# Grouped-query attention on one core: casts of two heads at a time, placed in gaps of GpSimd's plan

## The chip, the core and the metric

The kernel runs on one core of a Trainium2 chip. Its time is the device time in microseconds, here the median of three runs. A core has five engines with queues of their own: TensorE (PE in the profile, its weight loads PEld), VectorE (DVE), ScalarE (ACT), GpSimd (POOL) and SyncE (SP), which here only issues transfers. Each engine runs its own instructions in order; semaphores order them among each other.

## The reference

Batch 8, 8 heads of q, 2 key groups (k and v), 1024 rows, head size 64, all float32. Four heads of q share a group:

```python
scores = scale * np.matmul(q_group, k_group.transpose(0, 1, 3, 2))
scores_max = np.max(scores, axis=-1, keepdims=True)
attn = np.exp(scores - scores_max)
attn = attn / (np.sum(attn, axis=-1, keepdims=True) + 1e-08)
output[:, q_start:q_end, :, :] = np.matmul(attn, v_group)
```

## The kernel before

There are 64 jobs, j = 0 to 63: one head of q of one batch each. A job has eight pairs of score matmuls (L853), each of which fills a slot of 128 x 1024 float32 in PSUM; there are three slots. The exponential of a slot is made by one of two engines. ScalarE does it in one activation (L863, "act"). VectorE does it in steps: a linear pass out of PSUM into 16-bit integers whose bits are a rough exponential (L874, "dpass"), then, over a chain of two such slots (2048 columns), the mantissa bits (L881, "zh"), the exponent bits (L888, "two") and a product that corrects the mantissa (L897, "mul"). The exponent part `et` and the corrected part `zt` then both enter the second matmul with v (L915, "pv"). In the last TAIL heads a fourth step (L902, "add") adds the two on VectorE, so that TensorE needs one matmul per tile there and not two. Each group of seven pieces of the result is divided by its sums on VectorE (reciprocal L980, multiplication L989) and stored by SyncE (L993).

How many of a head's eight slots VectorE takes at most is its quota (L150): `FIRST[j]` for the first heads, then `MXD` and one more where `j % MORE == MORE // 2`.

The order of all of this is written out before the kernel is built. `Plan` plays the engines against each other with fixed costs (the `M_` constants in nanoseconds: `M_ACT` is one activation) and, where TensorE has a choice, plays each alternative `HORIZON` nanoseconds ahead and takes the one with the least idle time of ScalarE and VectorE. The events of the plan, sorted by planned time, become the instructions of each engine in that order.

GpSimd takes a part of the product step off VectorE. `Plan.gpsimd` (L208) does this only beside VectorE's pass out of PSUM (and the normalisation that may follow it): it opens a window of that length, first lets in a placement of v (`gplace`, L654) if one is due, then as many columns of a waiting product as fit (`gmul`, L827), at most `GWINS` parts per chain, for chains of heads 2 to 58. The rest of the columns stays with VectorE (L897). Each part waits for the VectorE instruction issued just before the window, so that it doesn't start sooner (L830). The plan itself counts no cast.

The matmuls need q and k transposed and in bfloat16. For this GpSimd issues transfers that cast one head of q (`cast_q`, L621) or one key group (`cast_k`, L634) from float32 in HBM to a bfloat16 tensor `qd` or `kd` in HBM, 128 KB each; SyncE then issues a transposing transfer of it into SBUF (`turn_q`, `turn_k`), 11 us and 12.5 us ahead of the first use by the plan. A cast is due 18 us (q) or 19 us (k) ahead (L762, L769). Once GpSimd's parts have begun, a due cast goes into the list `casts`. It leaves it right after a part if the next part with a later planned time starts over 2300 ns after this one's planned time, or, when it is 3000 ns overdue, at whatever event comes next. In both cases it waits for the score matmul that was last put in order (L809). The lines that decide this:

```python
    begun = [e[0] for e in ev if e[1] in ("gmul", "gplace")]
...
        if casts and casts[0][0] < when - 3000:
            cast(*casts.pop(0)[1:])
...
            later = [t for t in begun if t > when]
            if casts and (not later or later[0] > when + 2300):
                cast(*casts.pop(0)[1:])
```

Of the kernel before, what the change touches and what calls it, by code (L numbers as in the profile page):

```python
# [23 lines left out]
M_SWITCH = 99  # L24
M_MM = 30.3
M_PVTAIL = 180
M_ACT = 923
M_ATAIL = 107
M_FIX = 66
M_DTAIL = 80  # L30
# [6 lines left out]
M_GLEAD = 160  # L37
M_GFIX = 120
M_GCOL = 2.09
# [2 lines left out]
M_NORM = 531  # L42
M_HOLD = 2500
M_SPARE = 500

M_GAP = 90
M_RUNWAY = 1800
# [1 line left out]
M_WAIT = 250  # L49
M_TOL = 300  # L50

HORIZON = 8000
W_A = 1.0
W_D = .28
W_P = 0
# [1 line left out]
INF = float("inf")  # L57
# [1 line left out]
NPIECE = 8  # L59
GRAIN = 3  # L60
MXD = 2
MORE = 5
TAIL = 3
CHN = 2
LONG = 6
FIRST = (2, 1, 1)
GWINS = 2
GFROM = 2
GTO = 5
# [64 lines left out]
class Plan:  # L134
# [5 lines left out]
    def __init__(self, nj, npt, nct, nyt):  # L140
# [8 lines left out]
        self.qready = [M_START] + [M_START + M_Q1 + M_QSTEP * j for j in range(nj - 1)]  # L149
        self.quota = [FIRST[j] if j < len(FIRST) else MXD + (j % MORE == MORE // 2) for j in range(nj)]  # L150
        s = State()
# [42 lines left out]
    def act(self, s):  # L194
# [5 lines left out]
        else:  # L200
            _, sl, j, c = s.aq.pop(0)
            s.note(t, "act", sl, j, c)
            s.idleA += t - s.endA
            s.tA = s.endA = t + M_ACT
            s.slot[sl] = s.tA + M_ATAIL + M_SEE
# [33 lines left out]
    def dve(self, s):  # L239
# [13 lines left out]
        elif s.dq and s.dq[0][0] <= t and not (norm and t - s.norms[0][0] > M_HOLD):  # L253
            _, sl, j, c = s.dq.pop(0)
            n = len(STEPS) if j >= nj - TAIL else 3
            if s.open and s.open.nsteps != n:
# [23 lines left out]
        else:  # L280
# [5 lines left out]
            for ch in s.chains:  # L286
# [3 lines left out]
                if ch.at == 2 and ch.nsteps == 3 and ch.cols and ch.wins < GWINS:  # L290
                    if GFROM <= ch.pairs[0][0] < nj - GTO:
                        if s.dq and s.dq[0][0] < t + M_SPARE:
                            continue
# [47 lines left out]
    def choices(self, s):  # L341
# [10 lines left out]
        free = [x for x in (0, 1, 2) if s.slot[x] <= t]  # L352
        runway = s.tA - t + M_ACT * len(s.aq)
        slack = runway - cold * M_PAIR - M_PTAIL - (M_SWITCH if s.mode != "s" else 0)
# [70 lines left out]
    def pe(self, s, kind):  # L425
        t, nj = s.tP, self.nj
        if kind in "AD":
# [12 lines left out]
            else:  # L440
                s.dcount[j] += 1
                if j == 0:
                    s.twice.append(c)
                if j < nj - TAIL:
                    s.mms[j] += 1
# [78 lines left out]
    def run(self, s):  # L524
        while not s.end:
# [3 lines left out]
            kind, others = self.choices(s)  # L529
            if others and HORIZON:  # L530
                best = self.cost(s.copy(), kind, t + HORIZON)
                for x in others:
                    c = self.cost(s.copy(), x, t + HORIZON)
                    if c < best - 1:
# [8 lines left out]
def kernel(  # L543
# [7 lines left out]
    nc = tc.nc  # L551
    FP32 = mybir.dt.float32
    BF16 = mybir.dt.bfloat16
# [5 lines left out]
    B, H, S, D = q.shape  # L559
    G = k.shape[1]  # L560
# [3 lines left out]
    HS = S // 2  # L564
    NJ = B * H
# [12 lines left out]
    dram = ctx.enter_context(tc.tile_pool(name="dram", bufs=1, space=bass.MemoryType.DRAM))  # L578
# [39 lines left out]
        nc.vector.memset(t[:, :, :, D : D + 1], 1.0)  # L618
    kt, qt, qd, kd, vs = {}, {}, {}, {}, {}

    def cast_q(j):  # L621
        b, h = divmod(j, H)
        t = dram.tile([HS, 2 * D], BF16, name=f"qd{j}")
        qd[j] = t
        if j == NJ - 1:
            return nc.gpsimd.dma_start(
                out=t.rearrange("(c p) d -> p c d", p=128), in_=rows(q[b, h], True)
            )
        return nc.gpsimd.dma_start(  # L629
            out=t.rearrange("(a x) d -> a (x d)", x=4),  # L630
            in_=q[b, h].rearrange("(a x) d -> a (x d)", x=8),
        )

    def cast_k(b, g):  # L634
        t = dram.tile([HS, 2 * D], BF16, name=f"kd{b}_{g}")
        kd[(b, g)] = t
        return nc.gpsimd.dma_start(  # L637
            out=t.rearrange("(a x) d -> a (x d)", x=4),
            in_=k[b, g].rearrange("(a x) d -> a (x d)", x=8),
        )  # L640

    def rows(x, fours=False):
        how = "(p c two) d -> p c (two d)" if fours else "(c p two) d -> p c (two d)"
        return x.rearrange(how, p=128, two=2)
# [49 lines left out]
    load(nc.sync, "k", 1, NH)  # L696
    load_v(0, 0)
    cast_q(1)
    make_identity(nc, ident)
    cast_q(2)  # L700

    new_bank(0)
# [37 lines left out]
    for c in range(NH):  # L740
        for half in range(2):
            lo = half * D
# [4 lines left out]
    h = HS // 2  # L747
# [7 lines left out]
    ev = list(plan.ev)  # L755
    n = len(ev)
    for j in range(NJ):
        b, h = divmod(j, H)
        at = need[j]
        g = h // HPG  # L760
        if h % HPG == 0 and j:
            ev.append((at - 19000, "ck", None, (b, g), None))  # L762
            ev.append((at - 12500, "tk", None, (b, g), None))
            ev.append((at - 4000, "cp", None, (b, g), None))
            ev.append((places[j // HPG] - 8000, "lv", None, (b, g), None))
        if j == 0:
            ev.append((M_START + 100, "pl", None, (b, g), None))
        if j > 2:
            ev.append((at - 18000, "cq", None, j, None))  # L769
        if j > 1:  # L770
            ev.append((at - 11000, "tq", None, j, None))
    for x in [e for e in plan.ev if e[1] == "norm"]:
        lo, hi = x[2]
# [9 lines left out]
    now = None  # L783
# [3 lines left out]
    def flat(t):  # L787
        return t.bitcast(BF16).rearrange("p i a b -> p (i a b)")

    def terms(j, par, only=range(NC)):  # L790

        for ci in only:
            c = ci if par == 0 else (ci + NH) % NC
            if (j, c) in where:
                ch, i = where[(j, c)]
                if j < NJ - TAIL:
                    yield ci, et[ch].bitcast(BF16)[:, i, par, :]
# [1 line left out]
            elif (j, c) in pt:  # L799
                yield ci, pt[(j, c)][:, par, :]  # L800

    begun = [e[0] for e in ev if e[1] in ("gmul", "gplace")]
    casts = []
    vec, gps = None, None

    def cast(kind, j):
        ins = cast_k(*j) if kind == "ck" else cast_q(j)
        if now:
            tc.add_manual_dep(ins.ins, now.ins.name, Sync, reason="loads in time, not sooner")  # L809

    for when, kind, x, j, c, *cols in ev:
        if casts and casts[0][0] < when - 3000:
            cast(*casts.pop(0)[1:])
        if kind in ("ck", "cq"):

            if gps is None:
                cast(kind, j)
            else:
                casts.append((when, kind, j))
        elif kind in ("gmul", "gplace"):  # L820
# [3 lines left out]
            else:  # L824
                lo, w = c
                z = flat(zt[j])[:, lo : lo + w]
                gps = nc.gpsimd.tensor_tensor(  # L827
                    out=z, in0=flat(yt[j])[:, lo : lo + w], in1=z, op=ALU.mult
                )
            tc.add_manual_dep(gps.ins, vec.ins.name, Sync, reason="VectorE needs the port before")  # L830

            later = [t for t in begun if t > when]
            if casts and (not later or later[0] > when + 2300):
                cast(*casts.pop(0)[1:])
        elif kind == "tk":
            turn_k(*j)
        elif kind == "cp":
# [7 lines left out]
        elif kind == "score":  # L845
            b, h = divmod(j, H)
            t = kt[(b, h // HPG)]
            where_s[(j, c)] = new_slot(x)

            for half in range(2):  # L850
                lo = half * D
                ci = (c + NH * half) % NC
                now = nc.tensor.matmul(  # L853
                    sps[x][:, half, :],
                    lhsT=t[lo : lo + D, c // NH, ci % NH * 128 : (ci % NH + 1) * 128],
                    rhs=qt[j][lo : lo + D, 0, :],
                    start=True,
                    stop=True,
                )
# [9 lines left out]
        elif kind == "dpass":  # L869
            ch, i = j  # L870
            where[c] = j
            if i == 0:
                yt[ch] = yp.tile([128, CHN, 2, HS], U16, name="yt")
            vec = nc.vector.tensor_scalar(  # L874
                out=yt[ch][:, i, :, :], in0=where_s[c],
                scalar1=EXP_A, scalar2=EXP_B, op0=ALU.mult, op1=ALU.add,
            )
        elif kind == "zh":
# [3 lines left out]
                out=zt[j][:, 0:c], in0=yt[j][:, 0:c], scalar1=0x7F, scalar2=0x3F00,  # L882
                op0=ALU.bitwise_and, op1=ALU.bitwise_or,
            )
        elif kind == "two":
# [3 lines left out]
                out=et[j][:, 0:c], in0=yt[j][:, 0:c], scalar1=0x7F80, scalar2=None,  # L889
# [5 lines left out]
        elif kind == "mul":  # L895
            z = flat(zt[j])[:, 0 : cols[0]]
            vec = nc.vector.tensor_tensor(  # L897
                out=z, in0=flat(yt[j])[:, 0 : cols[0]], in1=z, op=ALU.mult
            )
        elif kind == "add":  # L900
            z = zt[j].bitcast(BF16)[:, 0:c]
            vec = nc.vector.tensor_tensor(  # L902
                out=z, in0=et[j].bitcast(BF16)[:, 0:c], in1=z, op=ALU.add
            )
        elif kind == "pv":
            job, piece = divmod(x, NPIECE)
            b, h = divmod(job, H)
            qs, par = divmod(piece, 2)
            lo = (x - plan.groups[plan.group_of[x]][0]) * (D + 1)
# [14 lines left out]
        elif kind == "pvf":  # L924
# [4 lines left out]
            for i in range(NPIECE):  # L929
# [3 lines left out]
                lo = i % 4 * (D + 1)  # L933
# [9 lines left out]
        elif kind == "pvl":  # L943
            b, h = divmod(NJ - 1, H)
# [3 lines left out]
            for i in range(NPIECE):  # L948
# [4 lines left out]
                lo = i % 4 * (D + 1)  # L953
# [9 lines left out]
        elif kind in ("rec", "norm"):  # L963
            lo, hi = x
            n = hi - lo
# [24 lines left out]
        elif kind == "store":  # L990
            b, h = divmod(j, H)
            r = place_of(j * NPIECE)
            ins = nc.sync.dma_start(  # L993
                out=rows(out[b, h], j in (0, NJ - 1)),
                in_=ost[:, r : r + NPIECE, :].rearrange("p (s two) d -> p s (two d)", two=2),
# [32 lines left out]
```

## Time and profile before

| | |
|---|---|
| median of three runs | 362.16 us (362.12 to 362.54) |
| the profiled execution | 361.83 us, of which the span is 360.1 us |
| exponentials on ScalarE (L863) | 374, 346.7 us busy |
| passes on VectorE (L874) | 138, 167.3 us busy |
| products on GpSimd (L827) | 91, 101.8 us busy |
| casts of q (L626, L629) and of k (L637) | 63 and 15 |
| issue to landing of a cast | q 3.5 us, k 3.4 us (medians) |

The span runs from the first to the last instruction of the core; the time of a run is a little longer. Busy time counts an engine's instructions without double counting where one begins before the last has ended; the mean of one instruction therefore can be longer than the distance from one start to the next. Of VectorE that distance is the better price: its instructions overlap by about 0.08 us.

### The profile page before, as it was taken

Reading aid. Unit: us, or ns where it says so; the run is one execution under the profiler, and the core shown is the slowest. Engines: PE = TensorE matmul, PEld = TensorE weight load, DVE = VectorE, ACT = ScalarE, POOL = GpSimd, SP = SyncE. Lnnn points to the kernel's source line nnn. Section 1 sums busy time; section 2 is a strip of 40 time slices with the busy share of each in tenths; the row PEclk is TensorE's granted clock in tenths of the full one; section 3 lists DMA queues with packets and bytes.
Section 4 is the critical chain, followed back from the end, with each engine's and each line's share of the span. In section 5 each row is a group of like instructions: output and inputs, shape, how many; then the busy total and the mean of one; then the engine's idle time right before and its main releaser. Section 6 shows DMA issues by size and latency. Waiting matters only on the chain.

```text
span 360.1 us, 14126 instructions
## 1 busy us (share of the span) xinstructions
PE 349.0 (97%) x6214; PEld 222.7 (62%) x6214; DVE 350.8 (97%) x511; ACT 349.3 (97%) x378; POOL 156.0 (43%) x191
## 2 busy tenths in 40 slices
PE   8889999999999999999999999999999999999995
PEld 3456666666666666666666666666665666566664
DVE  4999999999999999999999999999999999999995
ACT  5999999999999999999999999999999999999993
POOL 4124452452544365562466554664545344342000
PEclk9999999999999999999999999999999999999999
DMA  8847595674747868487676866657487755854123
GB/s 191 131 84 125 105 191 122 105 135 103 164 102 130 167 99 161 97 136 165 114 120 119 165 133 111 148 111 144 94 120 144 180 98 88 158 120 76 46 60 120
DMA packets 89406, 44.83 MB, mean 125 GB/s; under 512 B 46000, under 2 KB 87600, under 8 KB 88112
## 3 DMA queue, kind: packets, MB, share of 16 engines
q1 hardware_dynamic: 86208, 33.44, 40.8%
q0 software_dynamic: 2992, 10.23, 21.7%
q8 instruction: 48, 0.79, 0.9%
q10 hardware_dynamic: 144, 0.26, 0.2%
q14 instruction: 14, 0.11, 0.1%
HBM read 25.17 MB, written 27.00 MB: 145 GB/s over the span
## 4 chain that ended last, share of the span: by engine, by line
DVE 65%; PE 30%; issue 4%; DVEq 0%
DVE yt L874 32%; PE ops L915 15%; PE sp L853 13%; DVE zt L897 11%; DVE et L888 7%; DVE ost L989 7%; DVE zt L881 6%; DVE rec L980 2%; PE ops L708 1%; DVE zt L902 1%; PE sp L955 1%; PE sp L731 0%; PE ops L743 0%; PE ops L731 0%; DVE warm L616 0%
## 5 line engine op out<-in xcount | busy, mean ns | idle before, releaser
L863 ACT ACTIVATE pt<-sp 128x1024 bf16<-128x1024 f32 x374 | 346.7, 1034 | 1.8 <-PE sp L853 1.1
L853 PE MATMUL sp<-qt,kt 64*128 64x512 bf16 x1024 | 175.0, 384 | 5.0 <-DVE yt L874 2.9
L915 PE MATMUL ops<-va,pt 128*128 128x65 bf16 x2896 | 177.3, 194 | 0.0
L874 DVE TENSOR_SCALAR yt<-sp 128x1024 uint16<-128x1024 f32 x138 | 167.3, 1212 | 0.8 <-PE sp L853 0.8
L915 PEld LDWEIGHTS <-pt 128*128 128x128 bf16 x2896 | 128.4, 97 | 37.8 <-issue 37.8
L827 POOL TENSOR_TENSOR zt<-yt,zt 128x416 bf16<-128x416 bf16 (+3 forms) x91 | 101.8, 1118 | 101.8 <-DVE zt L881 47.5
L915 PE MATMUL ops<-va,zt 128*128 128x65 bf16 x1072 | 126.4, 194 | 0.2 <-DVE zt L897 0.2
L915 PE MATMUL ops<-va,et 128*128 128x65 bf16 x1032 | 119.1, 194 | 0.0
L915 PEld LDWEIGHTS <-et 128*128 128x128 bf16 x1032 | 81.1, 98 | 20.3 <-issue 20.3
L915 PEld LDWEIGHTS <-zt 128*128 128x128 bf16 x1072 | 85.3, 97 | 13.5 <-issue 13.2
L853 PEld LDWEIGHTS <-kt 64*128 64x128 bf16 x1024 | 47.8, 93 | 54.6 <-issue 33.6
L897 DVE TENSOR_TENSOR zt<-yt,zt 128x960 bf16<-128x960 bf16 (+6 forms) x70 | 62.0, 887 | 0.0
L629 POOL DMA_DIRECT2D qd<-in_q_dram x62 | 36.6, 591 | 32.4 <-PE sp L853 27.5
L881 DVE TENSOR_SCALAR zt<-yt 128x2048 uint16<-128x2048 uint16 x70 | 46.7, 670 | 0.3
L888 DVE TENSOR_SCALAR et<-yt 128x2048 uint16<-128x2048 uint16 x70 | 46.4, 664 | 0.0
L989 DVE TENSOR_TENSOR ost<-ops,rec 128x448 f32<-128x448 f32 (+2 forms) x73 | 44.3, 607 | 0.2
L654 POOL CAST va<-vs 128x512 bf16<-128x512 f32 x16 | 9.8, 611 | 21.8 <-DVE ost L989 6.8
L637 POOL DMA_DIRECT2D kd<-in_k_dram x15 | 9.2, 612 | 14.5 <-PE sp L853 14.5
L980 DVE RECIPROCAL rec<-ops 128x7 f32<-128x7 f32 (+2 forms) x73 | 14.1, 193 | 0.0
L708 PE MATMUL ops<-warm 128*128 128x128 bf16 (+1 forms) x30 | 5.2, 311 | 1.7 <-DVE warm L616 1.2
L708 PEld LDWEIGHTS <-warm 128*128 128x128 bf16 x30 | 2.4, 111 | 5.1 <-issue 4.0
L902 DVE TENSOR_TENSOR zt<-et,zt 128x2048 bf16<-128x2048 bf16 (+1 forms) x4 | 4.3, 1072 | 0.0
(37 smaller groups left out, 24.7 us busy)
## 6 DMA issues: line engine op xcount, KB each, us to landing
out_dram<-ost SPq DMA_DIRECT2D x64, 256.0 KB, 2.9
qd<-in_q_dram POOLq DMA_DIRECT2D x63, 128.0 KB, 3.5
vs<-in_v_dram SPq DMA_DIRECT2D x16, 256.0 KB, 4.4
kd<-in_k_dram POOLq DMA_DIRECT2D x15, 128.0 KB, 3.4
kt<-kt SPq DMA_DIRECT2D x30, 64.0 KB, 3.5
qt<-qd SPq DMA_TRANSPOSE x63, 3.7
q<-in_q_dram ACTq DMA_DIRECT2D x1, 256.0 KB, 2.9
kt<-kd SPq DMA_TRANSPOSE x15, 4.3
```

Source lines behind the costliest of these rows:

```text
L629: return nc.gpsimd.dma_start(out=t.rearrange("(a x) d -> a (x d)", x=4), in_=q[b, h].rearrange("(a x) d -> a (x d)", x=8),)
L708: nc.tensor.matmul(ops[bank][:, lo : lo + cols], lhsT=warm[:, 0:128], rhs=warm[:, 0:cols], start=not beside, stop=True, skip_group_check=b ...
L827: gps = nc.gpsimd.tensor_tensor(out=z, in0=flat(yt[j])[:, lo : lo + w], in1=z, op=ALU.mult)
L853: now = nc.tensor.matmul(sps[x][:, half, :], lhsT=t[lo : lo + D, c // NH, ci % NH * 128 : (ci % NH + 1) * 128], rhs=qt[j][lo : lo + D, 0, ...
L863: exps.append(nc.scalar.activation(out=p, in_=where_s[(j, c)], func=AF.Exp, scale=scale))
L874: vec = nc.vector.tensor_scalar(out=yt[ch][:, i, :, :], in0=where_s[c], scalar1=EXP_A, scalar2=EXP_B, op0=ALU.mult, op1=ALU.add,)
L881: vec = nc.vector.tensor_scalar(out=zt[j][:, 0:c], in0=yt[j][:, 0:c], scalar1=0x7F, scalar2=0x3F00, op0=ALU.bitwise_and, op1=ALU.bitwise_or,)
L888: vec = ins = nc.vector.tensor_scalar(out=et[j][:, 0:c], in0=yt[j][:, 0:c], scalar1=0x7F80, scalar2=None, op0=ALU.bitwise_and,)
L897: vec = nc.vector.tensor_tensor(out=z, in0=flat(yt[j])[:, 0 : cols[0]], in1=z, op=ALU.mult)
L915: nc.tensor.matmul(ops[plan.group_of[x] % 2][:, lo : lo + D + 1], lhsT=p[:, qs * 128 : (qs + 1) * 128], rhs=va[(b * G + h // HPG) % NVA][: ...
L980: vec = nc.vector.reciprocal(out=to, in_=sums)
L989: vec = nc.vector.tensor_tensor(out=to, in0=o, in1=by, op=ALU.mult)
```

## The change

A cast takes two heads of q in one transfer: heads 1, 2 and 63 stay alone, and every odd j from 3 to 61 brings head j+1 with it. The two key groups of a batch come in one transfer too, apart from the first batch's. The transfer keeps 128 rows on each side, each twice as long; the two heads are slices of one tensor in HBM, and the transposes are unchanged.

Casts leave the list by another rule. After each part of GpSimd, the planned time at which GpSimd is free is worked out from that part's cost. While the planned start of the next part, whatever its time, is later than that by more than `M_ISSUE` (650 ns), a cast is issued there, without waiting for a score, and 650 ns are added. A cast that is more than 5000 ns overdue goes out at the next event, with the wait, as before.

The plan's constants change too, so the whole order is another one: `M_ACT`, `HORIZON`, the quotas (`MORE`, `FIRST`) and `TAIL`.

```diff
-M_ACT = 923
+M_ACT = 917
+M_ISSUE = 650
-HORIZON = 8000
+HORIZON = 5500
-MORE = 5
-TAIL = 3
+MORE = 6
+TAIL = 4
-FIRST = (2, 1, 1)
+FIRST = (2, 1)
...
+    def cast(src, t):
+        return nc.gpsimd.dma_start(
+            out=t.rearrange("(a x) d -> a (x d)", a=128),
+            in_=src.rearrange("(a x) d -> a (x d)", a=128),
+        )
+
     def cast_q(j):
         b, h = divmod(j, H)
-        t = dram.tile([HS, 2 * D], BF16, name=f"qd{j}")
-        qd[j] = t
         if j == NJ - 1:
+            t = qd[j] = dram.tile([HS, 2 * D], BF16, name=f"qd{j}")
             return nc.gpsimd.dma_start(
                 out=t.rearrange("(c p) d -> p c d", p=128), in_=rows(q[b, h], True)
             )
-        return nc.gpsimd.dma_start(
-            out=t.rearrange("(a x) d -> a (x d)", x=4),
-            in_=q[b, h].rearrange("(a x) d -> a (x d)", x=8),
-        )
+        n = 2 if j > 2 else 1
+        t = dram.tile([n * HS, 2 * D], BF16, name=f"qd{j}")
+        for i in range(n):
+            qd[j + i] = t[i * HS : (i + 1) * HS, :]
+        return cast(q.rearrange("b h s d -> (b h s) d")[j * S : (j + n) * S, :], t)
 
     def cast_k(b, g):
-        t = dram.tile([HS, 2 * D], BF16, name=f"kd{b}_{g}")
-        kd[(b, g)] = t
-        return nc.gpsimd.dma_start(
-            out=t.rearrange("(a x) d -> a (x d)", x=4),
-            in_=k[b, g].rearrange("(a x) d -> a (x d)", x=8),
-        )
+        n = G - g
+        t = dram.tile([n * HS, 2 * D], BF16, name=f"kd{b}_{g}")
+        for i in range(n):
+            kd[(b, g + i)] = t[i * HS : (i + 1) * HS, :]
+        lo = (b * G + g) * S
+        return cast(k.rearrange("b g s d -> (b g s) d")[lo : lo + n * S, :], t)
...
-            ev.append((at - 19000, "ck", None, (b, g), None))
+            if g == 0 or b == 0:
+                ev.append((at - 19000, "ck", None, (b, g), None))
...
-        if j > 2:
+        if j > 2 and (j % 2 or j == NJ - 1):
             ev.append((at - 18000, "cq", None, j, None))
...
-    begun = [e[0] for e in ev if e[1] in ("gmul", "gplace")]
+    begun = [e for e in ev if e[1] in ("gmul", "gplace")]
+    starts = [e[0] + M_GLEAD for e in begun] + [INF]
+    nth, free = 0, 0
...
-    def cast(kind, j):
+    def begin(kind, j, gate):
         ins = cast_k(*j) if kind == "ck" else cast_q(j)
-        if now:
+        if now and gate:
             tc.add_manual_dep(ins.ins, now.ins.name, Sync, reason="loads in time, not sooner")
...
-        if casts and casts[0][0] < when - 3000:
-            cast(*casts.pop(0)[1:])
+        if casts and casts[0][0] < when - 5000:
+            begin(*casts.pop(0)[1:], True)
...
-            later = [t for t in begun if t > when]
-            if casts and (not later or later[0] > when + 2300):
-                cast(*casts.pop(0)[1:])
+            took = 614 if kind == "gplace" else M_GFIX + M_GCOL * c[1]
+            free = max(free, when + M_GLEAD) + took
+            nth += 1
+            while casts and starts[nth] > free + M_ISSUE:
+                begin(*casts.pop(0)[1:], False)
+                free += M_ISSUE
```

More of the change, by code (lines that the diff above doesn't have):

```diff
@@ L800, in terms @@
                 yield ci, pt[(j, c)][:, par, :]
-    begun = [e[0] for e in ev if e[1] in ("gmul", "gplace")]
+    begun = [e for e in ev if e[1] in ("gmul", "gplace")]
+    starts = [e[0] + M_GLEAD for e in begun] + [INF]
+    nth, free = 0, 0
     casts = []
     vec, gps = None, None
-    def cast(kind, j):
+    def begin(kind, j, gate):
         ins = cast_k(*j) if kind == "ck" else cast_q(j)
-        if now:
+        if now and gate:
             tc.add_manual_dep(ins.ins, now.ins.name, Sync, reason="loads in time, not sooner")
     for when, kind, x, j, c, *cols in ev:
-        if casts and casts[0][0] < when - 3000:
-            cast(*casts.pop(0)[1:])
+        if casts and casts[0][0] < when - 5000:
+            begin(*casts.pop(0)[1:], True)
         if kind in ("ck", "cq"):
             if gps is None:
-                cast(kind, j)
+                begin(kind, j, True)
             else:
```

## The prediction

> **What bounds the kernel now.** I read the page's busy shares first. Three engines stand at 97% of the span, so the shares alone can't say which one sets the end:
>
> ```profile
> PE 349.0 (97%) x6214; PEld 222.7 (62%) x6214; DVE 350.8 (97%) x511; ACT 349.3 (97%) x378; POOL 156.0 (43%) x191
> ```
>
> Next the table of waits, for VectorE (DVE) and then ScalarE (ACT). Columns: who <- for whom, us in total, times, longest.
>
> ```profile
> DVE q L719 <- DMA q<-in_q_dram: 2.4, 1, 2.4
> ...
> DVE yt L874 <- PE sp L853: 0.8, 2, 0.5
> DVE rec L980 <- PE sp L955: 0.6, 1, 0.6
> ```
>
> ```profile
> ACT pt L863 <- PE sp L853: 1.1, 3, 0.6
> ```
>
> VectorE's waits all lie in the first 9 us, except the 0.6 us ahead of the last reciprocal. By the timeline it has no other gap of over 50 ns from 8.5 to 355.1 us. ScalarE's row of the page has 374 exponentials, 346.7 us busy, 0.927 us each. By their starts, nine in ten follow the last one after 0.90 to 0.93 us, 0.918 in the mean of these, so 374 x (0.927 - 0.918) = 3.4 us, plus its own 1.1 us of waits, is time in which ScalarE stood late, about 4.5 us. TensorE has slack that the busy share hides: by the starts of L853, some pairs of score matmuls come 0.39 us and more apart where an unhindered pair takes 0.22. So the end is set by the sum of VectorE's work; ScalarE could follow some 4.5 us sooner before it became the bound.
>
> Then VectorE's instructions by shape, to see whether its work runs at its own price. The product (L897) has these rows:
>
> ```profile
> L897 DVE TENSOR_TENSOR zt<-yt,zt 128x960 bf16<-128x960 bf16 x21 | 13.9, 661 | 0.0
> ...
> L897 DVE TENSOR_TENSOR zt<-yt,zt 128x1216 bf16<-128x1216 bf16 x9 | 6.9, 769 | 0.0
> ...
> L897 DVE TENSOR_TENSOR zt<-yt,zt 128x1248 bf16<-128x1248 bf16 x5 | 5.2, 1039 | 0.0
> ```
>
> 1248 columns cost 1039 ns where 1216 cost 769. That is no price of the shape: three of the five were held up. The timelines of GpSimd (POOL) and VectorE show by what. At 318 us:
>
> ```profile
> 317.55 0.61 POOL L654 CAST va<-vs 128x512 bf16<-128x512 f32 x1 [0.75 <-DVE et L888]
> 318.10 0.55 POOL L629 DMA_DIRECT2D qd<-in_q_dram  x1
> 318.67 0.92 POOL L827 TENSOR_TENSOR zt<-yt,zt 128x384 bf16<-128x384 bf16 x1
> ```
>
> ```profile
> 317.41 1.21 DVE L874 TENSOR_SCALAR yt<-sp 128x1024 uint16<-128x1024 f32 x1
> 318.54 0.61 DVE L989 TENSOR_TENSOR ost<-ops,rec 128x448 f32<-128x448 f32 x1
> 319.07 1.20 DVE L897 TENSOR_TENSOR zt<-yt,zt 128x1248 bf16<-128x1248 bf16 x1
> 320.19 1.21 DVE L874 TENSOR_SCALAR yt<-sp 128x1024 uint16<-128x1024 f32 x1
> ```
>
> The plan gave GpSimd one window (the PSUM pass L874 and the normalisation L989) for a placement of v and a product part. The cast of q was issued between the two, so the part ran from 318.67 to 319.59, past the window's end at 319.07, and VectorE's product took 1.12 us to the next start in place of 0.72.
>
> **What the Trainium skill says.** SBUF - State Buffer, "SBUF: two separate sides": VectorE and GpSimd share a pair of SBUF ports; an instruction of VectorE with two SBUF inputs or in a two-port mode, and one of GpSimd, exclude each other for the whole instruction. The trace agrees: L897 loses about 0.4 us beside a late part, L874 (PSUM input) keeps its 1.13 us beside 60 parts. DMA: Bandwidth & Descriptors, "SWDGE vs HWDGE vs iDMA": a cast in flight must be issued by GpSimd, which writes its descriptors into SBUF and is locked out in the same way. The trace agrees: casts take 486 ns alone and up to 900 ns beside VectorE's two-port work, while no instruction of VectorE is longer beside a cast alone. The same page, "Anatomy of one DMA": about 2.0 us plus bytes over 436 GB/s; doubling a cast from 128 to 256 KB written adds 0.3 us by that, to the 3.5 us to landing that the page shows.
>
> **Part by part.**
>
> *Collisions removed.* I went through all starts of L897, L881 and L888 and compared each with its shape's usual distance to the next start. Eight are late, each beside a product part that had been pushed back by a cast: L897 at 79.77 (+0.42), 257.50 (+0.22), 262.35 (+0.40), 271.22 (+0.42), 295.49 (+0.41) and 319.07 (+0.41), and L881 at 112.53 (+0.10) and 292.51 (+0.11). Sum 2.49 us. Of the 78 casts 18 are followed at once by a product; 8 of those cost something. The old rule leaves out a part with the same planned time (t > when), which is how a cast came between placement and product, and lets a late cast in anywhere, behind a TensorE score. The new one takes the next part by its index and asks for 650 ns of free plan. Between the 107 parts of GpSimd, 101 of 106 gaps are over 650 ns, the median 2.0 us, so few casts should grow 5 us old and fall back on the gated path. I take all eight as gone: -2.49 us, on VectorE, hence on the path.
>
> *Fewer casts.* q: heads 1, 2, 63 alone and 30 pairs, 33 for 63; k: 8 for 15. So 37 fewer of about 0.57 us, 21 us of GpSimd, which is 43% busy: worth nothing by itself. The price of a double cast isn't in the trace. It keeps 128 rows on each side, twice as long: at least 0.49 to 0.55 us as now, at most 1.1 if time goes with bytes. The cast of head 63 (L626), with more and shorter rows, took 0.81. I take 0.55; at 1.1 it would outrun 650 ns, and 30 of the 106 gaps lie between 0.65 and 1.1 us.
>
> *Waits and queues.* The casts lose their wait for a score (27.5 + 14.5 us for q and k), behind which only GpSimd's next parts queue. SyncE's transposes (63 + 15, unchanged) wait for casts 58.6 us now, and stores queue behind them; the only cost of this to TensorE is 0.4 us. A cast planned 18 us ahead and at most 5 late lands some 8 us before need. Nothing.
>
> *Split of heads.* Quotas for VectorE before: 2+1+1, then 2 each and 3 where j mod 5 is 2 (12 heads): 138. After: 2+1, then 2 each and 3 where j mod 6 is 3 (11 heads): 138. So 374 exponentials and 138 passes stay.
>
> *TAIL 4.* Heads 60 to 63 take the fourth step: 2+2+2+3 = 9 pairs in place of 7, one more addition (L902) of 2048 columns, +1.13 us from start to next start; TensorE drops 16 matmuls at 30 ns, 0.5 us. VectorE's one late gap (0.6 us) might absorb half. Between +0.5 and +1.13; I take +1.13.
>
> *New plan.* M_ACT 917 is nearer the 0.918 us seen than 923. The number of columns that GpSimd takes follows from the plan and can't be read from the trace: now 91 parts, 58 x 416 + 26 x 672 + 5 x 384 + 2 x 704 = 44,928 columns. One column is worth (1133 - 565) / (2048 - 960) = 0.52 ns of VectorE. The chains that may be shared (heads 2 to 58) have 124 pairs under both quotas. I take no change; +-5 parts of 494 columns is +-1.3 us.
>
> Sum: -2.49 + 1.13 = -1.4 us. Against the profiled execution's own 361.83 us (span 360.1 and 1.7 around it) that is 360.4; that execution is 0.33 us below the median of 362.16, so the forecast is 360.7 us. The 0.2% that can be told from no change is 0.7 us.
>
> **Rivals.** *More than that* (12%): ScalarE's late 4.5 us allow it, if the new plan also hands over some 5 parts more: 360.7 - 1.3 = 359.4. *It cancels* (17%): double casts cost near 1.1 us and outrun tight gaps, or late ones still fall into windows; four new collisions of 0.41 eat 1.4 us: 362.2. For it: 30 tight gaps, and casts stretch to 0.9 us beside VectorE even now. Against: there are half as many casts, each takes the first gap that is wide enough, and its overrun is only the part above 650 ns. *Slower* (26%): a shorter look-ahead (HORIZON 5500) and other quotas give an order with fewer shared windows in heads 2 to 58. From 5 to 6 lost parts (1.4 / 0.257) it is no gain, from 9 slower than the bound; a loss of 12 gives 360.7 + 12 x 494 x 0.52 ns = 363.8. For it: only 91 of at most 124 parts are used, so the number is loose, and the plan counts no cast, so nothing balances it against them; against: passes, pairs and window lengths are the same.
>
> **How the numbers follow.** Forecast 45% (360.0 to 361.4), more 12%, cancels 17%, slower 26%. Faster 0.57 is forecast and more together; same 0.17; slower 0.26. The range reaches from 358.8, at 7 to 8 parts gained, to 363.8, where 12 are lost.
>
> **What would show it.** Right: no L897 or L881 beside a late L827; about 41 casts, each behind a part and 0.5 to 0.6 us long; the row of L902 at four of 2048 columns; no new wait of VectorE. Wrong: L629 near 1 us with products at once behind; the columns of L827 well under 44,928; gaps of VectorE before L874; SyncE's late transposes stopping scores.

## The result and the profile after

The changed kernel takes 358.81 us (median of 4 runs, 357.89 to 359.50) against 362.14 us. The ratio is 0.9907, 95% interval 0.9882 to 0.9932: 3.3 us faster, where 1.4 were forecast. The profiled execution took 358.87 us, its span is 357.0. The page's first part after the change:

```profile
PE 345.1 (97%) x6196; PEld 221.2 (62%) x6196; DVE 347.9 (97%) x512; ACT 347.3 (97%) x378; POOL 149.8 (42%) x161
```

VectorE has one instruction more and 2.9 us less busy time. Its waits (who <- for whom, us, times, longest) are as few as before:

```profile
DVE q L724 <- DMA q<-in_q_dram: 2.9, 1, 2.9
DVE yt L885 <- PE sp L864: 1.0, 2, 0.5
DVE warm L617 <- PEq L1023: 0.9, 1, 0.9
DVE rec L991 <- PE sp L966: 0.3, 1, 0.3
```

So the time came out of VectorE's own work. (The second row's two waits are 0.5 us each, at 8.1 and 10.6 us; the later one is new.) The groups by shape (busy us, mean ns | idle before) show which:

```profile
L835 POOL TENSOR_TENSOR zt<-yt,zt 128x416 bf16<-128x416 bf16 x56 | 54.6, 974 | 56.3 <-DVE et L899 21.6 <-DVE zt L892 16.2 <-PE sp L864 5.4
L835 POOL TENSOR_TENSOR zt<-yt,zt 128x672 bf16<-128x672 bf16 x35 | 50.9, 1455 | 47.8 <-DVE et L899 30.5 <-DVE zt L892 9.0 <-DVE zt L908 4.3
...
L908 DVE TENSOR_TENSOR zt<-yt,zt 128x960 bf16<-128x960 bf16 x30 | 18.9, 630 | 0.0
...
L913 DVE TENSOR_TENSOR zt<-et,zt 128x2048 bf16<-128x2048 bf16 x4 | 4.8, 1202 | 0.0
L835 POOL TENSOR_TENSOR zt<-yt,zt 128x704 bf16<-128x704 bf16 x3 | 4.6, 1517 | 7.2 <-DVE rec L991 6.6 <-DVE et L899 0.6
L835 POOL TENSOR_TENSOR zt<-yt,zt 128x384 bf16<-128x384 bf16 x4 | 3.6, 909 | 0.0
L908 DVE TENSOR_TENSOR zt<-yt,zt 128x1248 bf16<-128x1248 bf16 x3 | 2.3, 780 | 0.0
```

GpSimd's parts are now 98, and more of them are wide: 56 x 416 + 35 x 672 + 3 x 704 + 4 x 384 = 50,464 columns, 5,536 more than the 44,928 before. Before, the first two of these rows were:

```profile
L827 POOL TENSOR_TENSOR zt<-yt,zt 128x416 bf16<-128x416 bf16 x58 | 56.4, 972 | 61.4 <-DVE et L888 24.3 <-DVE zt L881 23.5 <-DVE ost L989 6.7
L827 POOL TENSOR_TENSOR zt<-yt,zt 128x672 bf16<-128x672 bf16 x26 | 37.8, 1453 | 37.6 <-DVE zt L881 22.6 <-DVE et L888 13.6 <-DVE zt L897 1.4
```

At 0.52 ns a column the difference is 2.9 us less for VectorE. The held-up products are gone too: 1248 columns take 780 ns where their mean was 1039, 960 take 630 where it was 661. The fourth addition of 2048 columns (L913) is there, at 1.13 us from start to start.

But three other VectorE instructions are held up now, by 1.07 us in all. At 250 us, GpSimd and then VectorE in the timeline:

```profile
250.60 0.61 POOL L659 CAST va<-vs 128x512 bf16<-128x512 f32 x1 [3.56 <-DMA vs<-in_v_dram]
```

```profile
250.71 1.04 DVE L892 TENSOR_SCALAR zt<-yt 128x2048 uint16<-128x2048 uint16 x1
251.68 1.21 DVE L885 TENSOR_SCALAR yt<-sp 128x1024 uint16<-128x1024 f32 x1
```

A placement of v began outside its window, as soon as its load had landed, and the mantissa step beside it took 0.97 us to the next start, not 0.60. Why the load was late stands in the timelines of GpSimd's and SyncE's issues shortly before:

```profile
236.40 0.55 POOL L623 DMA_DIRECT2D qd<-in_q_dram  x1 [7.49 <-PE sp L864]
238.85 0.49 POOL L623 DMA_DIRECT2D kd<-in_k_dram  x1 [1.90 <-PE sp L864]
```

```profile
236.56 0.38 SPq L1004 DMA_DIRECT2D out_dram<-ost  x1
242.16 1.16 SPq L677 DMA_TRANSPOSE qt<-qd  x1
243.47 1.14 SPq L667 DMA_TRANSPOSE kt<-kd  x1
244.71 0.53 SPq L656 DMA_DIRECT2D vs<-in_v_dram  x1
```

The cast of q at 236.40 went out with the wait for a score, which only overdue casts have. By the trace it landed at 242.10 and the cast of k at 243.46; SyncE's two transposes went out at 242.16 and 243.47, and SyncE issued nothing for 5 us before. The load of v stood behind them, and took 5.8 us to land, in flight with the next doubled cast (median of all loads: 3.8 us). In all, doubled casts take longer to land than single ones before (3.5 us for q, 3.4 for k):

```profile
qd<-in_q_dram POOLq DMA_DIRECT2D x30, 256.0 KB, 4.6
...
kd<-in_k_dram POOLq DMA_DIRECT2D x7, 256.0 KB, 5.0
```

SyncE's waits for casts of q, before and then after (us, times, longest), add up to about as much, but the longest has grown:

```profile
SPq L672 <- DMA qd<-in_q_dram: 58.6, 30, 4.8
```

```profile
SPq L677 <- DMA qd<-in_q_dram: 61.0, 20, 6.6
```

Of the 15 placements after the first, three began 0.12 us after their load had landed (122.9, 164.4 and 250.6 us); each lies at one of the three held-up instructions, the one at 122.9 by pushing back the product behind it.

VectorE's sum from the two profiles: columns -2.88, collisions -2.48 and +1.07, the addition +1.13, its waits after 9 us +0.26 (0.58 to 0.84), together -2.9 us; its last instruction ends 2.8 us sooner (353.8 for 356.6). From there to the end of the span it is another 0.2 us shorter (3.24 for 3.46), which I can't explain.

### The profile page after: what moved, and what is told of

It reads as the page before. It is cut to its first block, busy times and chain, and to the rows that moved or that the text cites. A ratio compares the mean times of both kernels' runs of the same rounds, so it can differ in the third digit from the quotient of the medians.

```text
span 357.0 us, 13990 instructions
## 1 busy us (share of the span) xinstructions
PE 345.1 (97%) x6196; PEld 221.2 (62%) x6196; DVE 347.9 (97%) x512; ACT 347.3 (97%) x378; POOL 149.8 (42%) x161
## 4 chain that ended last, share of the span: by engine, by line
ACT 49%; PE 28%; DVE 18%; DMA 2%; issue 2%; DVEq 0%; POOLq 0%
ACT pt L874 49%; PE ops L926 15%; PE sp L864 12%; DVE yt L885 9%; DVE zt L908 3%; DVE et L899 2%; DVE ost L1000 2%; DVE zt L892 1%; DMA qt<-qd 1%; DMA qd<-in_q_dram 1%; PE sp L966 1%; DVE rec L991 1%; DVEq L899 0%; POOLq L1023 0%
## 5 line engine op out<-in xcount | busy, mean ns | idle before, releaser
L864 PE MATMUL sp<-qt,kt 64*128 64x512 bf16 x1024 | 172.6, 382 | 5.7 <-DVE yt L885 1.6
L926 PE MATMUL ops<-va,pt 128*128 128x65 bf16 x2904 | 175.3, 194 | 0.0
L835 POOL TENSOR_TENSOR zt<-yt,zt 128x416 bf16<-128x416 bf16 (+3 forms) x98 | 113.7, 1160 | 111.3 <-DVE et L899 52.8
L926 PE MATMUL ops<-va,et 128*128 128x65 bf16 x1016 | 117.5, 194 | 0.0
L908 DVE TENSOR_TENSOR zt<-yt,zt 128x960 bf16<-128x960 bf16 (+7 forms) x70 | 56.4, 807 | 0.0
L892 DVE TENSOR_SCALAR zt<-yt 128x2048 uint16<-128x2048 uint16 (+1 forms) x70 | 47.6, 680 | 0.3
L899 DVE TENSOR_SCALAR et<-yt 128x2048 uint16<-128x2048 uint16 (+1 forms) x70 | 46.7, 673 | 0.0
L623 POOL DMA_DIRECT2D qd<-in_q_dram x32 | 21.1, 658 | 20.2 <-PE sp L864 19.4
L623 POOL DMA_DIRECT2D kd<-in_k_dram x8 | 5.3, 666 | 6.9 <-PE ops L926 4.9
L913 DVE TENSOR_TENSOR zt<-et,zt 128x2048 bf16<-128x2048 bf16 (+1 forms) x5 | 5.5, 1100 | 0.0
```

Of the source, the lines that this page charges most:

```text
L623: return nc.gpsimd.dma_start(out=t.rearrange("(a x) d -> a (x d)", a=128), in_=src.rearrange("(a x) d -> a (x d)", a=128),)
L835: gps = nc.gpsimd.tensor_tensor(out=z, in0=flat(yt[j])[:, lo : lo + w], in1=z, op=ALU.mult)
L864: now = nc.tensor.matmul(sps[x][:, half, :], lhsT=t[lo : lo + D, c // NH, ci % NH * 128 : (ci % NH + 1) * 128], rhs=qt[j][lo : lo + D, 0, ...
L892: vec = nc.vector.tensor_scalar(out=zt[j][:, 0:c], in0=yt[j][:, 0:c], scalar1=0x7F, scalar2=0x3F00, op0=ALU.bitwise_and, op1=ALU.bitwise_or,)
L899: vec = ins = nc.vector.tensor_scalar(out=et[j][:, 0:c], in0=yt[j][:, 0:c], scalar1=0x7F80, scalar2=None, op0=ALU.bitwise_and,)
L908: vec = nc.vector.tensor_tensor(out=z, in0=flat(yt[j])[:, 0 : cols[0]], in1=z, op=ALU.mult)
```

## The experiments

The change has three parts that can be set apart, since the plan counts no cast: the plan's constants, the rule for gaps, and the doubled casts. The first four runs undo or do one each. Times are medians, set against runs of the kernel before on the same chip. The runs took place on three chips, on which the kernel before took 361.8 to 362.2 us.

**Casts alone, old plan.** The changed kernel with the five constants of before:

```diff
-M_ACT = 917
-HORIZON = 5500
-MORE = 6
-TAIL = 4
-FIRST = (2, 1)
+M_ACT = 923
+HORIZON = 8000
+MORE = 5
+TAIL = 3
+FIRST = (2, 1, 1)
```

> The old plan's constants with the new casts (two heads at a time, only in gaps). Theory: casts and plan add up; VectorE's products stay at 44,928 columns given to GpSimd, and only collisions go. About 2.5 us less than before if they all go, 1.4 less if v loads come late here too: 359.6 to 360.8 us, 91 product parts, chain of waits still VectorE. Rival, the plan does it all and the casts are hidden: within 0.5 us of before.

Measured: 360.87 us, ratio 0.9962 (0.9949 to 0.9976), 91 parts. Less than 2.5 us, though only two collisions (0.8 us) are left. A wait that I hadn't named came in at the start:

```profile
8.18 1.23 DVE L885 TENSOR_SCALAR yt<-sp 128x1024 uint16<-128x1024 f32 x1 [0.48 <-PE sp L864]
9.44 0.69 DVE L892 TENSOR_SCALAR zt<-yt 128x2048 uint16<-128x2048 uint16 x1
11.65 1.22 DVE L885 TENSOR_SCALAR yt<-sp 128x1024 uint16<-128x1024 f32 x1 [1.52 <-PE sp L864]
```

VectorE stood for 1.5 us at 11.65, because TensorE's score waited 1.73 us for a transposed q. SyncE's first transpose went out at 6.27 us here, at 4.81 in the kernel before. Whether the doubled casts, in flight with the single one it needs, made that late isn't shown. For it: with single casts on the same plan and rule (third run) VectorE waits 0.2 us at that place. Against it: in the thirteenth run the casts are single and the first transpose goes out as late, at 6.06 us, and in the fifth they are doubled and it goes out at 4.90.

A second cause shows in TensorE's granted clock. Three of the seven executions, the profiled one among them, have a mean of 0.995 and take 361.3 to 361.7 us; the other four take 360.1 to 360.9. In the profile the clock is 0.50 from 12.5 to 15.9 us, and VectorE waits another 0.5 us for a score at 17.0.

**Plan alone, old casts.** The kernel before with the five new constants.

> The new plan's constants with the old casts (one head each, old rule). Theory: 5,536 more columns on GpSimd are worth 2.9 us of VectorE, the fourth step costs 1.1, collisions stay as many as before: about 1.8 us less than before, 360.4 us, with 98 product parts and some eight late VectorE instructions. Rival, the casts do it all: 362 to 363 us.

Measured: 359.24 us, ratio 0.9920 (0.9908 to 0.9933), 98 parts with 50,464 columns, nine collisions of 2.6 us. So 2.85 us come from the plan alone. That this equals the columns' price of 2.9 is in part luck. In the profiles VectorE's last instruction ends 2.05 us sooner (354.55 for 356.59): the columns take off 2.9, the addition puts on 1.1, and waits shrink by 0.5, which is 2.3, or 0.2 too much. The rest, 0.47 us, lies between that instruction and the end of the span (2.99 us for 3.46), and I don't know why.

**Rule alone: old plan, single casts.** The kernel before with the part of the diff from `begun` on and `M_ISSUE`.

> The old plan and single casts, with the new rule of gaps alone. Theory: the rule, not the doubling, removes the collisions: about 2 to 2.5 us less than before, no L897 beside a late product. Rival, it takes fewer casts, and 78 of them find too few gaps, so that many grow overdue: less than 1 us.

Measured: 359.90 us, ratio 0.9941 (0.9930 to 0.9952), 2.2 us less. Five products of 1248 columns, and none of them held up:

```profile
L903 DVE TENSOR_TENSOR zt<-yt,zt 128x1248 bf16<-128x1248 bf16 x5 | 4.0, 794 | 0.0
```

Three collisions (0.85 us) are left in its profile. The rule did it, without fewer casts, and at least as well as rule and doubling together (360.87, with intervals that just overlap). Of the 2.2 us, 1.6 are collisions; in the profiles 0.46 us again lie behind VectorE's last instruction.

**Doubling alone: old plan, old rule.** The new `cast`, `cast_q`, `cast_k` and due events, with the old constants and the old rule.

> The old plan and the old rule, with casts of two heads or both groups. Theory: half as many casts, so about half as many collisions: 1 to 1.3 us less than before. Rival, it is the number of casts that counts: 2 us or more less. Rival, double casts hold GpSimd for longer: no gain.

Measured: 361.01 us, ratio 0.9974 (0.9967 to 0.9981): 1.1 us less. Four collisions of 1.1 us remain of eight of 2.5; again VectorE stands 1.4 us at 11.3 us for a score.

The second four start from the changed kernel.

**Loads of v sooner.**

```diff
-            ev.append((places[j // HPG] - 8000, "lv", None, (b, g), None))
+            ev.append((places[j // HPG] - 12000, "lv", None, (b, g), None))
```

> The changed kernel with each load of v ordered 12 us ahead of its placement, not 8. Theory: the three late VectorE instructions left in the changed kernel (1.07 us) come from placements that begin right as their load lands, since the loads queue on SyncE behind transposes that wait for casts; with the earlier loads these go: 357.7 to 358.2 us, about 0.3% below the changed kernel. Rival, the three have another cause, or the earlier loads push transposes back: 358.8 us or more.

Measured: 357.49 us, ratio 0.9876 (0.9863 to 0.9888). No collision is left. The placement that had begun at 250.60 now waits for VectorE's place and not for its load:

```profile
249.04 0.61 POOL L659 CAST va<-vs 128x512 bf16<-128x512 f32 x1 [2.58 <-DVE zt L892]
```

The interval overlaps that of the changed kernel a little, but the profile shows the cause gone and 1.07 of the 1.3 us.

**Thirteen product parts given back to VectorE.** Each of 416 columns, the last part of its chain; the plan's order is kept:

```diff
-            z = flat(zt[j])[:, 0 : cols[0]]
+            w = cols[0] + (back[j][4][1] if j in back else 0)
+            z = flat(zt[j])[:, 0 : w]
```

> The changed kernel, in which 13 product parts of 416 columns, spread over the kernel, go back from GpSimd to VectorE; the order and the places of the casts stay. Theory: VectorE's work is the bound, so 5,408 columns at 0.52 ns are paid in full: 2.8 us more, 361.6 us. Rival, ScalarE has become the bound of the changed kernel (49% of its chain of waits) and VectorE has room: under 1.4 us more.

Measured: 359.99 us, ratio 0.9950 (0.9932 to 0.9968): only 1.2 us more. It doesn't say what a column is worth: in its profile two other things had gone by the way, the three collisions (there is another one, of 0.2 us, for their 1.07) and the 0.5 us gap of VectorE at the start.

**TAIL back at 3.**

> The changed kernel with TAIL back at 3: one addition of 2048 columns less on VectorE, 16 matmuls of 30 ns more on TensorE; the rest of the order stays up to the last heads, with the same columns on GpSimd. Theory as predicted: 0.5 to 1.1 us less than the changed kernel, 357.7 to 358.3 us. Rival, the end is set by TensorE's matmuls after the last exponential, and the fourth step pays: 0.3 us more or beyond.

Measured: 358.48 us, ratio 0.9906 (0.9883 to 0.9928): no difference that can be told. As its profile happens to show no collision, the fourteenth run asks the same in a version that has none.

**Single casts with new plan and rule.** `n = 1` in both casts, an event for each.

> The changed kernel with one head or one group per cast again, new plan and new rule kept: 78 casts. Theory: the rule removes the collisions without the doubling, and single casts land sooner at the start and hold SyncE up less: 0.5 to 1.5 us less than the changed kernel, 357.3 to 358.3 us. Rival, with 98 parts the gaps don't hold 78 casts, so that many grow overdue and collide: 358.8 us or more.

Measured: 357.12 us, ratio 0.9876 (0.9854 to 0.9898), with 78 casts, one collision of 0.14 us. Of the later loads of v only one lands within 2 us of its placement; in the changed kernel six do. Two of the six executions have a mean granted clock of 0.995 and take 358.9 and 359.0 us, the other four 356.6 to 357.2.

The next four:

**Early loads, and parts given back.** The edits of the fifth and the sixth run, `lv` and `back`, together.

> The kernel with v loads 12 us ahead (357.5 us) with the same 13 product parts given back to VectorE. There are no collisions in it that giving parts back could remove by the way. Theory: the 5,408 columns are paid in full on VectorE, 2.8 us: 360.3 us. Rival, ScalarE bounds this kernel and VectorE has some room: 1.2 us or less more, 358.7 us.

Measured: 361.19 us, ratio 0.9977 (0.9963 to 0.9992), but this median lies between two groups. By TensorE's mean granted clock the 22 executions fall into halves. The 11 at 0.997 and above take 359.7 to 360.9 us, 360.16 at the median; the 11 at 0.988 to 0.995 take 361.4 to 363.0. The first half is 2.7 us above early loads alone (357.49, all four executions at 0.997 and above), nearly the 2.8 of the columns. The profiled execution (362.62, 0.988) belongs to the other half. Its row of the granted clock, and that of early loads alone, in slices of 9 us:

```profile
PEclk9969999999999999999999999999999999999998
```

```profile
PEclk9999999999999999999999999999999999999998
```

TensorE waits 2.3 us for a transposed q, and its clock is then 0.50 from 17.5 to 24.3 us. VectorE stands 1.8 us for a score up to 18.4 and 1.3 us for TensorE again up to 26.1. What lets the clock fall isn't shown.

**Single casts, early loads.**

> New plan, new rule, one head or group per cast, v loads 12 us ahead: the version that should beat both kernels. Theory: with early v loads no collision is left in either form, so single casts gain only what doubled ones lose at the start, 0.4 us: 356.8 to 357.2 us. Rival, the doubling costs by itself all along the kernel: 356 us or less. Rival, the early loads were the same thing seen twice and 78 casts are too many: 357.5 us or more.

Measured: 357.13 us, ratio 0.9863 (0.9850 to 0.9875): with the single casts at 357.12 the fastest of all. Early loads bring nothing there; they mend only what the doubling had made late. The table of waits shows no wait of VectorE after the start but this one, and ScalarE's chain has grown (line of the page, chain that ended last):

```profile
DVE rec L991 <- PE sp L966: 0.3, 1, 0.3
```

```profile
ACT 82%; PE 16%; issue 1%; DVE 1%
```

**M_ACT alone.** The kernel before with 917 for 923.

> The kernel before with M_ACT 917 in place of 923 and nothing else; the plan then gives GpSimd 96 parts with 48,704 columns, 3,776 more. Theory: 0.52 ns a column, so 2.0 us less than before, 360.1 us, with collisions about as many as before. Rival, it is the timing of the order and not the columns that the new constants bring: no more than 0.5 us less, or more than 2.5.

Measured: 360.89 us, ratio 0.9970 (0.9959 to 0.9982): 1.3 us of the 2.0. The columns are there, 96 parts with 48,704 in all, and ten collisions of 2.6 us, about as much as before:

```profile
L827 POOL TENSOR_TENSOR zt<-yt,zt 128x416 bf16<-128x416 bf16 x60 | 58.4, 973 | 61.2 <-DVE zt L881 34.9 <-DVE ost L989 10.7 <-DVE et L888 9.1
L827 POOL TENSOR_TENSOR zt<-yt,zt 128x672 bf16<-128x672 bf16 x30 | 43.7, 1457 | 31.8 <-DVE et L888 20.6 <-DVE zt L881 10.4 <-DVE zt L897 0.6
```

Most of the rest went into the end: VectorE's last reciprocal waits 1.2 us for TensorE where it waited 0.6.

**The next part by its index, nothing else of the rule.**

```diff
-            later = [t for t in begun if t > when]
+            nth += 1
+            later = begun[nth:]
```

> The kernel before, in which the next part is taken by its index, so that a placement and a product of the same window count as neighbours; the 2300 ns, the wait for a score and the 3000 ns stay. Theory: only the collisions between a placement and a product go (79.8, 295.5 and 319.1 us in the profile before, 1.2 us), so about half of what the whole rule brings: 360.8 to 361.2 us. Rival, the index is all of the rule: 360 us. Rival, casts pushed on grow overdue and collide elsewhere: 361.8 us or more.

Measured: 360.69 us, ratio 0.9965 (0.9952 to 0.9978): 1.5 us of the rule's 2.2. The three collisions behind placements are gone, the other five are there (1.25 us). So the index accounts for 1.2 of the 1.5 us. The product of 1248 columns is the line to look at:

```profile
L899 DVE TENSOR_TENSOR zt<-yt,zt 128x1248 bf16<-128x1248 bf16 x5 | 4.0, 797 | 0.0
```

Three more runs settled what was open.

**Parts given back, in the version with single casts and early loads.**

> The version with new plan, new rule, single casts and early v loads (357.1 us, no collision and no gap of VectorE after the start), with 13 product parts given back to VectorE. Theory: the bound is the larger of VectorE's and ScalarE's work; VectorE gets 2.8 us more, ScalarE stands late less than 1 us there, so 2 to 2.8 us are paid: 359.1 to 359.9 us. Rival, ScalarE alone bounds: under 1.2 us more, 358.3 us or less.

Measured: 360.23 us, ratio 0.9953 (0.9939 to 0.9966): 3.1 us more, of which two new collisions are 0.5. So 2.6 of the 2.8 us are paid, starting from a version whose chain names ScalarE for 82%. (The two ran on different chips; by the ratios it is 3.3 us more. From start to start VectorE's products take 53.9 us in this profile and 51.3 in the other.)

**TAIL at 3, in the same version.**

> The same version with TAIL at 3. Theory, after the first try: VectorE's 1.13 us less turns into a wait of about 0.9 us more for TensorE's last matmuls, so within 0.4 us of 357.1 us. Rival, as predicted: 0.5 to 1.1 us less, 356.0 to 356.6 us.

Measured: 357.36 us, ratio 0.9872 (0.9859 to 0.9885), beside 357.13: no difference. VectorE's last wait shows where the saved addition goes:

```profile
DVE rec L991 <- PE sp L966: 1.2, 1, 1.2
```

The wait is 1.2 us, not 0.3: with TAIL 3 VectorE has 1.13 us less to do, and at the end waits 0.9 us longer for TensorE.

**New plan and doubling, old rule.**

> The new plan with doubled casts and the old rule, the cell still missing between plan, rule and doubling. Theory: with the old rule doubling removes half of the collisions but costs up to 0.5 us at the start: 0.5 to 1.1 us less than plan alone (359.24 us), 358.1 to 358.7 us, so that the new rule brings little or nothing once casts are doubled. Rival, plan, rule and doubling simply add: doubling costs 1.7 us also here, 360.9 us.

Measured: 358.51 us, ratio 0.9906 (0.9889 to 0.9923), with four collisions of 1.0 us in the profile. With that all eight cells are there (medians in us):

| | single, old rule | single, new rule | double, old rule | double, new rule |
|---|---|---|---|---|
| old plan | 362.1 | 359.9 | 361.0 | 360.9 |
| new plan | 359.2 | 357.1 | 358.5 | 358.8 |

The plan is worth 2.1 to 2.9 us in every column, and the rule 2.1 to 2.2 us with single casts; all these pairs have intervals that stand apart. With doubled casts no effect of the rule can be told.

Of the doubling only one cell stands by itself: it gains 1.1 us on the old plan under the old rule. On the new plan under the old rule it gains 0.7, and under the new rule it loses 1.0 (old plan) and 1.7 (new plan), but in these three pairs the intervals overlap. The granted clock is a part of it. In the executions at 0.997 and above the medians for the old and the new plan are 359.9 and 356.9 with single casts under the new rule, 360.3 and 358.8 with doubled ones: losses of 0.4 and 1.9. The loss on the new plan rests also on the traces: where the changed kernel has three collisions (1.07 us) and a wait of 0.5 us at 10.6, the version with single casts has one collision of 0.14 us.

Executions at 0.995 or less are 22 of 75 in the versions with doubled casts (11 of them from the ninth run), 2 of 40 in those with single casts, and none of the 75 of the kernel before that ran beside them. So the doubling may also cost time by this way; no run here sets it apart.

## Why the prediction was too small

The direction was right, the size wasn't: -1.4 us forecast, -3.3 measured.

- *What bounds the kernel* held. VectorE's sum is what the time follows; columns given back came back into the time nearly in full. Of ScalarE's steps, three in four lie at 0.90 to 0.93 us, with a mean of 0.913; it takes 0.90 to 0.96 to hold nine in ten, with a mean of 0.917. The median gap between GpSimd's parts is 1.4 us; 2.0 is the mean. Neither changes the argument.
- *New plan* is the step that failed: "I take no change; +-5 parts of 494 columns is +-1.3 us". The price of a column was right and the count was not: there are seven parts more, and nine more of 672 columns than before; together they are 5,536 columns, 2.88 us. The rival "more than that" named the mechanism and made it half as large. I had treated the count as a draw around the old one. It wasn't: one constant alone, M_ACT nearer to ScalarE's measured pace, brought 3,776 of the columns. That the plan ran its ScalarE slower than the profile showed could be read beforehand; what follows for GpSimd's windows could not, short of playing the plan. But the plan is a part of the kernel that needs no chip: the expectation of the eleventh run names its columns beforehand.
- *TAIL 4*, +1.13 us, was mis-sized: it is nothing in time. The gap ahead of the last reciprocal, 0.6 us before, which I wrote "might absorb half", takes nearly all, as with TAIL 3 under the new plan that gap is 1.2 us. In VectorE's sum the 1.13 us stand; without them the wait at the end would have been longer by nearly as much.
- *Collisions removed*, -2.49 us: the eight did go. With single casts the rule is the cause (2.2 us by itself, 1.6 of them collisions); with doubled ones four were left of eight before the rule came in. But "I take all eight as gone" left out those that the change makes: the net was -1.41.
- *Waits and queues*, "Nothing", is where the new ones come from. The estimate of 0.3 us more for a doubled cast's landing, worked out from the Trainium skill's page DMA: Bandwidth & Descriptors, "Anatomy of one DMA", was too low: the profile of the changed kernel shows 4.6 us for q and 5.0 for both groups, where single ones took 3.5 and 3.4, and the measurement decides. "The casts lose their wait for a score" didn't come true either: the overdue ones keep it, and six waits of casts for TensorE, 31 us, are left of 45. With a cast allowed to be 5 us overdue, SyncE's longest wait for one grew from 4.8 to 6.6 us. "Lands some 8 us before need" already held this: the transpose is ordered 11 us ahead, so it waits some 3 us for such a cast at the head of SyncE's queue. I asked only whether a transpose comes too late for a score, not what stands behind the transpose in SyncE's queue: the load of v, and behind it GpSimd's placement.
- *The price of a double cast* on GpSimd was right: at least 486 ns as before, and for q 0.66 us in the mean, as long as single ones under the same plan and rule (0.65, eighth run). "It cancels" by casts of 1.1 us is out. "Slower" by lost parts is out too: the parts grew.

Right and wrong terms partly offset. In time, along the table: plan -2.9, rule -2.1, doubling under the new rule +1.7. That the far edge of the stated range fits, "358.8, at 7 to 8 parts gained", is part luck: seven parts were gained, but worth 2.9 us and not 1.8, and the new collisions took 1.1 us back.

What stays open: which other constants share in the remaining 1,760 columns, since only M_ACT was run alone; what lets TensorE's granted clock fall to 0.50 in the first 25 us of some executions, and whether doubled casts bring that about; and the 0.2 to 0.5 us behind VectorE's last instruction.

## What to carry to other kernels

When an engine has no gaps left, look at its instructions by shape: a shape whose mean is far above that of its neighbours in size is being held up, and the other engine's timeline at that moment shows by what. When a planner is given new costs, what it hands from one engine to another is a term of the sum as large as the edits beside it; don't enter it as zero with a small spread, and try each constant alone. Where executions of one kernel differ by more than the effect, sort them by granted clock before a wait in one profile is put down to the edit. Before transfers are merged, follow every queue that waits for one of them down to what stands behind it, since the bigger transfer can land later for all of them, as it did here.

## What I had not expected of the hardware

A doubled cast, 128 rows on either side of twice the length, costs GpSimd no more issue time (486 ns at the least in both) but lands 1.1 us (q) to 1.6 us (k) later. A placement of v on GpSimd, a single-input cast of 128x512, holds up VectorE's bit operations on 2048 columns just as a product does: 0.36 us at 250.7, where a product cost 0.29 at 123.9. In four of the 17 profiled executions (first, eighth, ninth and fifteenth run) TensorE's granted clock was 0.50 for one stretch of 3.4 or 6.8 us, starting between 12 and 21 us, and executions with a mean of 0.995 or less took 0.7 to 2.5 us longer than the others of the same kernel. And the share of an engine in the chain of waits is no measure of its weight where two engines are close: with 82% on ScalarE, work added to VectorE still came through almost whole.
